# Moving the compressed-input, query and key projections between the quarters of a state space stage, with weight tiles of their own for the compression

## The chip, the cores and the metric

The kernel runs on one core of a Trainium2 chip. The metric is the device time of one execution in microseconds (us). The five instruction streams in the text are PE (TensorE, matrix products), ACT (ScalarE), DVE (VectorE), POOL (GpSimd) and SP (SyncE, which here only issues transfers).

## What is computed

One block of a hybrid model over 512 tokens of width 1024. A state space mixer and an attention mixer read the same normalized input, their outputs are gated and merged, then a convolutional feed-forward network, a gated extra input and a last norm follow. The part that the change touches is this, cut from the reference:

```python
n1 = rmsnorm(h, g_mix[i])
z = n1 @ w_in[i]
y_ssm = s5_mixer(z[..., OFF_SSM:OFF_Q], ...)
y_nsa = nsa_mixer(z[..., OFF_Q:OFF_KV], z[..., OFF_KV:OFF_NSA_GATE], ...)

def compress_blocks(k, pe, w1, w2):
    ch = k.reshape(bsz, g, t // CMP_STRIDE, CMP_STRIDE, dh)
    blocks = jnp.concatenate([ch[:, :, :-1], ch[:, :, 1:]], axis=3) + pe
    flat = blocks.reshape(bsz, g, blocks.shape[2], CMP_BLOCK * dh)
    return jax.nn.gelu(flat @ w1) @ w2

kc = compress_blocks(k_cmp, pe_k, wk1, wk2)
vc = compress_blocks(v_cmp, pe_v, wv1, wv2)
```

The projection z of the attention side has 128-column pieces for compressed keys and values, four for queries and two for the keys of the two other branches.

## The kernel before, in words

**Projections.** `proj` (its matmuls are lines 83 to 85) takes a 128-column piece of `w_in`, 512 KB in float32, loaded by `wraw` (L183) into a raw tile `wr`. ACT rounds it into a high part `wh` (L76) and DVE or POOL writes the rest into a low part `wl` (L55). PE then does 24 matmuls of 128x512: eight slices of the width, three products each. The result lies in a PSUM bank `pj` with the tag `acc`, which has two banks, until ACT has copied it on. The pool `weights` keeps three buffers of `wr` and two each of `wh` and `wl`. In the text the projections are numbered in the order in which PE does them: 0 to 3 are the inputs of the state space mixer, 4 and 5 the compressed keys and values, 6 to 9 the queries (`QT`), 10 and 11 the other keys (`KK`), 12 to 15 the first merge gates (`t1a`).

**The state space stage** is four calls of `ssm_quarter`. Each builds block matrices `Z` (DVE, copied by ACT) and `CX` (POOL, copied by ACT), transposes `Z` on PE (`wbps`, L641), copies the two results to `WB` (ACT), multiplies them with the inputs (`wps`, L649), multiplies `CX` and `Z` (`tps`, L669, into a bank that ACT first fills with zeros, L665), runs scans on DVE, and ends in the outputs `yps` (L703, L706). The matmuls of this stage are small: 32 to 128 columns.

**The compression** copies projections 4 and 5 from PSUM into `FL` (four ACT copies each), multiplies them with the weights `cmp_wk1` and `cmp_wv1` (`hps`, L748, 16 blocks each, 64 columns, plain float32), and applies a gelu and a second small product (`kps`, L756 and L767). Its four weight pieces of 512 KB take buffers of the same tag `wr` (L745, L746).

**What sets the order.** The Tile framework schedules: it takes the program order as priority, simulates the engines with its own durations, and writes one fixed order per engine. Each engine runs its own order one instruction after another and waits where a semaphore asks for it. So the program order is not the order on the engines: in the schedule of before, projections 4 to 15 already lie between the pieces of the quarters, although the text of the program has them behind `ssm_quarter(3)`.

Of the kernel before, what the change touches and what calls it, by code (L numbers as in the profile page):

```python
# [9 lines left out]
F32 = mybir.dt.float32  # L10
F32R = mybir.dt.float32r
# [5 lines left out]
MUL, ADD, SUB = ALU.mult, ALU.add, ALU.subtract  # L17

P = 128
T = 512  # L20
# [4 lines left out]
HD = 64  # L25
NCMP = 32
# [10 lines left out]
OFF_KV = 1024  # L37
# [8 lines left out]
def hybrid_kernel(ctx: ExitStack, tc: tile.TileContext, A, out):  # L46
    nc = tc.nc
    V, G, S, PE = nc.vector, nc.gpsimd, nc.scalar, nc.tensor

    def dr(name, off, ap):  # L50
        t = A[name]
        return bass.AP(tensor=t.tensor, offset=t.offset + off, ap=ap)

    def tt(o, a, b, op, e=V):
        e.tensor_tensor(o, a, b, op=op)  # L55
# [19 lines left out]
    def copy(o, a):  # L75
        S.activation(o, a, AF.Copy)  # L76

    def split(hi, lo, src, e=V):
        copy(hi, src)
        tt(lo, src, hi, SUB, e)  # L80

    def mm3(ps, lh, ll, rh, rl, start, stop):
        PE.matmul(ps, lh, rh, start=start, stop=False)  # L83
        PE.matmul(ps, lh, rl, start=False, stop=False)  # L84
        PE.matmul(ps, ll, rh, start=False, stop=stop)  # L85

    def pool(name, bufs=1, side=None, space=None):
        kw = {"name": name, "bufs": bufs, "reuse_waits": "tile"}
        if side:
            kw["side"] = side  # L90
        if space is not None:
            kw["space"] = space
        return tc.tile_pool(**kw)

    cp = ctx.enter_context(pool("const"))
    pn = ctx.enter_context(pool("norm"))
    pw = ctx.enter_context(pool("weights", 2))
# [3 lines left out]
    def bank(tag, name):  # L101
        return psp.tile([P, 512], F32, tag=tag, name=name, bufs=BANKS[tag])

    def slot(p, tag, shape, dt, name):
        return p.tile(shape, dt, tag=tag, name=name, bufs=1)
# [5 lines left out]
    def small(tag, n=1, bufs=4):  # L111
        return cp.tile([P, n], F32, name=tag, tag=tag, bufs=bufs)
# [58 lines left out]
    def last(engine):  # L171
        return next(i for i in reversed(nc.cur_bb.bb.instructions) if i.engine == engine)
# [3 lines left out]
    def either():  # L176
        turn[0] ^= 1
        return ("acc", "o")[turn[0]]
# [7 lines left out]
    def wload(name, ld, row0, c0, kt, c, e=V, keep=None, raw=None):  # L186
        if raw is None:
            raw = wraw(name, ld, row0, c0, kt, c)
        if keep is None:
            hi = pw.tile([P, kt * c], F32R, name="wh", tag="wh").rearrange("p (k c) -> p k c", k=kt)  # L190
            lo = pw.tile([P, kt * c], F32R, name="wl", tag="wl").rearrange("p (k c) -> p k c", k=kt)
        else:
            hi, lo = keep
        split(hi, lo, raw, e)
        return hi, lo

    def proj(c0, e=V, w=None):
        hi, lo = w or wload("w_in", INW, 0, c0, KD, P, e)
        ps = bank("acc", "pj")
        for k in range(KD):  # L200
            mm3(ps, hi[:, k], lo[:, k], n1h[:, k], n1l[:, k], k == 0, k == KD - 1)
        return ps
# [6 lines left out]
    pa = sA.enter_context(pool("attn_in"))  # L209
    sY = ExitStack()  # L210
    py = sY.enter_context(pool("ssm_out", 1, "right"))
    t1a = slot(py, "t8", [P, 4, T], F32, "t1a")
    sS = ExitStack()
    pS = sS.enter_context(pool("ssm", 1, "right"))
    Uc = pS.tile([P, NPAIR, NCH], F32, name="Uc")
# [113 lines left out]
    with tc.manual_schedule(engines={mybir.EngineType.PE, mybir.EngineType.Activation, mybir.EngineType.DVE}):  # L329
# [26 lines left out]
        r = rstd_of(ss4[:, 2:4], n=2)  # L356
# [163 lines left out]
    FL = slot(pa, "ptc", [P, 2, 16, 2, NCMP], F32, "FL")  # L520
# [33 lines left out]
    for lv in range(5):  # L554
        n = 1 << lv
# [8 lines left out]
    tab_at = last(mybir.EngineType.Pool)  # L564
# [3 lines left out]
    with tc.issue_after(tab_at):  # L568
# [12 lines left out]
        blk = pa.tile([P, 4], F32, name="blk")  # L581
# [6 lines left out]
    for ct in range(4):  # L588
# [3 lines left out]
        for j in range(L):  # L592
            n = L - 1 - j
# [8 lines left out]
    sM = ExitStack()  # L602
# [104 lines left out]
        stt(un, un, dcol[:, q:q + 1], yps, MUL, ADD)  # L707
        S.activation(yT[:, q].rearrange(flat), un, AF.Gelu_apprx_tanh)

    for q in range(4):  # L710
        ssm_quarter(q)
    sM.close()
    sS.close()


    KK = slot(pa, "kv", [P, 2, 2, T], F32R, "KK")
    KC = pa.tile([P, 2, 2, 64], F32R, name="KC")
    VC = slot(pa, "v4", [P, 2, 4, 2, HD], F32R, "VC")
    W2 = pa.tile([P, 2, HD], F32, name="W2")
    nc.sync.dma_start(W2[:, 0], dr("cmp_wk2", 0, [[HD, P], [1, HD]]))  # L720
    nc.sync.dma_start(W2[:, 1], dr("cmp_wv2", 0, [[HD, P], [1, HD]]))
    W2d = pa.tile([P, 2, HD], F32, name="W2d")
    G.tensor_copy(W2d, W2[:, 0:1].to_broadcast([P, 2, HD]))
    for i in range(2):
        ps = proj(OFF_KV + i * P)
        f = FL[:, i]
        for g in range(2):
            for j in range(2):
                x = ps[64 * g:64 * g + 64, j:j + 1]
                copy(f[64 * j:64 * j + 64, :, g, 0:NCMP - 1],  # L730
                     bass.AP(tensor=x.tensor, offset=x.offset, ap=[x.ap[0], [2, 16], [16, NCMP - 1]]))
    QT = slot(cp, "h16", [P, 4, 2, T], F32R, "QT")
    for i in range(4):
        ps = proj(OFF_Q + i * P)
        split(QT[:, i, 0], QT[:, i, 1], ps)
    for br, c0 in ((0, OFF_KV + 256), (1, OFF_KV + 512)):
        ps = proj(c0)
        for g in range(2):
            s0, o0 = 64 * g, 64 * (1 - g)
            copy(KK[s0:s0 + 64, br, g], ps[s0:s0 + 64])  # L740
            tt(KK[o0:o0 + 64, br, g], ps[s0:s0 + 64], KK[s0:s0 + 64, br, g], SUB)
    for i, nm in enumerate(("cmp_wk1", "cmp_wv1")):
        hps = bank("acc", "hps")
        for c in range(2):
            w1 = pw.tile([P, 8, P], F32, name="w1", tag="wr", bufs=3)  # L745
            nc.sync.dma_start(w1, dr(nm, c * 1024 * P, [[P, P], [P * P, 8], [1, P]]))  # L746
            for k in range(8):
                PE.matmul(hps[:, 0:64], w1[:, k], FL[:, i, 8 * c + k].rearrange("p g n -> p (g n)"),  # L748
                          start=(c == 0 and k == 0), stop=(c == 1 and k == 7))
        kps = bank("s", "kps")  # L750
        h1 = pa.tile([P, 64], F32, name=f"hid{i}")
        pe = small("pe")
        copy(pe, hps[:, NCMP - 1:NCMP])
        S.activation(h1, hps[:, 0:64], AF.Gelu_apprx_tanh, bias=pe)
        if i == 0:
            PE.matmul(kps[:, 0:64], W2d.rearrange("p a d -> p (a d)"), h1, start=True, stop=True)  # L756
            with tc.issue_after(tab_at):
                G.memset(KC.bitcast(F32), 0.0)
            kv = kps[:, 0:64].rearrange("p (g n) -> p g n", g=2)
            for s in range(2):  # L760
                r = slice(64 * s, 64 * s + 64)
                split(KC[r, 0, :, 32 * s:32 * s + 32], KC[r, 1, :, 32 * s:32 * s + 32], kv[r])
        else:
            hid = pw.tile([P, 2, 4, NCMP], F32, name="hidv", tag="mg")
            V.tensor_copy(hid, h1.rearrange("p (g n) -> p g n", g=2)[:, :, None].to_broadcast([P, 2, 4, NCMP]))
            for g in range(2):
                PE.matmul(kps[:, 64 * g:64 * g + 64], hid[:, g].rearrange("p r n -> p (r n)"), W2[:, 1],  # L767
                          start=True, stop=True)
                vc = pw.tile([P, 4, HD], F32, name="vc", tag="mg")
                tt(vc, kps[:, None, 64 * g:64 * g + 64].to_broadcast([P, 4, HD]),  # L770
                   blk[:, :, None].to_broadcast([P, 4, HD]), MUL)
                split(VC[:, g, :, 0], VC[:, g, :, 1], vc)


    t1s = [t1a]
# [25 lines left out]
    for hc in range(2):  # L801
        hi, lo = wload("ssm_w_glu", SSMW, 0, hc * 256, 4, 256, V)
        for cc in range(2):
            c = 2 * hc + cc
            ps = bank(either(), "glu")
# [15 lines left out]
    class Unit:  # L821
# [7 lines left out]
        def queries(self, prev):  # L829
            if self.br:  # L830
                self.QQ = prev.QQ
            else:
                self.QQ = pt.tile([P, 2, T], F32R, name="QQ", tag="QQ")
                for half in range(2):
                    nc.sync.dma_start(self.QQ[64 * half:64 * half + 64].bitcast(F32),
                                      QT[self.r0:self.r0 + 64, self.i].bitcast(F32))

        def scores(self, qt):
            w = P * (qt + 1)
            ps = bank("s", "sps")  # L840
            for x in range(2):
                PE.matmul(ps[:, :w], self.QQ[:, x, qt * P:(qt + 1) * P], KK[:, self.br, self.g, :w],
                          start=x == 0, stop=x == 1)
# [18 lines left out]
        def values(self, kt, prev):  # L862
            g = self.g
            if kt == NQ - 1:
                self.ops = prev.ops if self.br else bank("o", "ops")
                if not self.br:
                    vc = VC[:, g, self.h % 4].rearrange("p x d -> p (x d)")
                    PE.matmul(self.ops, vc, PTC[:, 0, g], start=True, stop=False)
# [9 lines left out]
    def compressed(qt):  # L878
        qs_ = slice(qt * P, (qt + 1) * P)
        ps = bank("s", "cs")  # L880
        for i in range(4):
            mm3(ps[:, 64 * i:64 * i + 64], QT[:, i, 0, qs_], QT[:, i, 1, qs_], KC[:, 0, i // 2], KC[:, 1, i // 2],
                True, True)
# [114 lines left out]
    for d2 in range(4):  # L998
        hi, lo = wload("w_br_nsa", D, 0, d2 * 256, 4, 256, V)
        for dd in range(2):  # L1000
            dt_ = 2 * d2 + dd
            ps = bank(either(), "br")
            for k in range(4):
                c = dd * P
                mm3(ps, hi[:, k, c:c + P], lo[:, k, c:c + P], oS[:, 0, k], oS[:, 1, k], k == 0, k == 3)
            mg = t2()[:, dt_]
# [20 lines left out]
    ps = bank("s", "cvps")  # L1027
# [8 lines left out]
    for qp in range(2):  # L1036
        for hf, qt in ((0, 0), (0, 1), (1, 0), (1, 1)) if qp == 0 else ((0, 2), (1, 2), (0, 3), (1, 3)):
            cs = slice(hf * 512, hf * 512 + 512)
            qs_ = slice(qt * P, (qt + 1) * P)
            ps = bank(either(), "wo")  # L1040
# [117 lines left out]
    with pool("fin", 1, "right") as pz:  # L1158
# [20 lines left out]
        for hf in range(2):  # L1179
            for qt in range(NQ):  # L1180
# [6 lines left out]
                for i, (c0, w) in enumerate(pieces):  # L1187
                    pg = bank(either(), "pg")
                    c = slice(c0, c0 + w)
# [14 lines left out]
                if hf == 1:  # L1204
                    xn = pw.tile([P, D], F32, name="xf", tag="wr", bufs=3)
                    r = rstd_of(ss[qt][:, 0:1], ss[qt][:, x:x + 1])
# [39 lines left out]
```

## Time and profile before

| | us |
|---|---|
| median of 3 runs | 847.91 |
| lowest, highest | 847.84, 849.98 |
| the profiled execution | 850.72 |
| its span, first to last instruction | 849.0 |
| PE busy in it | 825.2 |
| DVE, ACT, POOL busy | 454.2, 377.7, 278.8 |

The profile is one execution, 2.81 us above the median of the runs. Its page says of each engine how long it was busy. [...]

### The profile page before, as it was taken

How to read it: one execution, taken by the hardware profiler on the slowest of the kernel's cores; microseconds unless marked ns; L12 is line 12 of the kernel's file. 1: busy time of each engine (PE TensorE's matmuls, PEld its weight loads, DVE VectorE, ACT ScalarE, POOL GpSimd, SP SyncE). 2: the span in 40 equal slices, each digit the busy share in tenths (PEclk: the TensorE clock that was granted, in tenths of full speed). 3: DMA queues.
4: the chain of work that ended last, by engine and by line, in shares of the span. 5: the costliest groups of instructions: out<-in, count | busy, mean ns of one | idle time of the engine just before them, and what ended most of it. 6: DMA issues, size and time to landing. Idle time of an engine off the chain costs nothing. (4 is left out here: it accounts for less than half of the span.)

```text
span 849.0 us, 12151 instructions
## 1 busy us (share of the span) xinstructions
PE 825.2 (97%) x4565; PEld 688.9 (81%) x4565; DVE 454.2 (53%) x968; ACT 377.7 (44%) x688; POOL 278.8 (33%) x314
## 2 busy tenths in 40 slices
PE   7998999999999999999999999999999999999996
PEld 5876888888888888878898888888888888888885
DVE  6898877348676750595454444444444212324535
ACT  4447533344776663344354444444444212333522
POOL 7485200214555444141033333333333221221341
PEclk9998998899999999999999999999999999999998
DMA  9363223531332522344032333333332223541202
GB/s 243 85 167 88 63 64 90 151 97 51 100 91 63 170 54 76 104 133 135 1 100 75 100 99 100 100 99 100 99 93 92 90 99 100 183 164 50 73 22 80
DMA packets 112000, 83.66 MB, mean 99 GB/s; under 512 B 9665, under 2 KB 97477, under 8 KB 111942
## 3 DMA queue, kind: packets, MB, share of 16 engines
q1 hardware_dynamic: 111262, 81.82, 33.3%
q10 hardware_dynamic: 680, 1.07, 0.3%
q8 instruction: 36, 0.59, 0.3%
q14 instruction: 22, 0.18, 0.1%
HBM read 75.54 MB, written 3.15 MB: 93 GB/s over the span
## 5 line engine op out<-in xcount | busy, mean ns | idle before, releaser
L55 POOL TENSOR_TENSOR wl<-wr,wh 128x1024 fp32r<-128x1024 f32 x49 | 118.2, 2413 | 346.2 <-ACT wh L76 320.5
L76 ACT ACTIVATE wh<-wr 128x1024 fp32r<-128x1024 f32 x101 | 106.8, 1058 | 124.8 <-PE dn L85 47.0
L55 DVE TENSOR_TENSOR wl<-wr,wh 128x1024 fp32r<-128x1024 f32 x52 | 66.8, 1284 | 87.7 <-ACT wh L76 87.7
L83 PE MATMUL pj<-n1h,wh 128*128 128x512 f32 x224 | 93.1, 416 | 0.8 <-ACT wh L76 0.8
L85 PE MATMUL pj<-n1h,wl 128*128 128x512 f32 x224 | 89.4, 401 | 0.2 <-DVE wl L55 0.2
L84 PE MATMUL pj<-n1l,wh 128*128 128x512 f32 x224 | 89.3, 399 | 0.0
L64 DVE SCALAR_TENSOR_TENSOR cv<-ub,cvp,cv 128x511 f32<-128x511 f32 (+1 forms) x44 | 32.9, 748 | 70.6 <-ACT cv L1075 69.8
L84 PE MATMUL ua<-n2l,wh 128*128 128x512 f32 (+1 forms) x176 | 67.0, 381 | 0.4 <-DVE n2l L64 0.4
L83 PE MATMUL ua<-n2h,wh 128*128 128x512 f32 (+1 forms) x176 | 67.0, 380 | 0.2 <-ACT n2h L167 0.2
L83 PE MATMUL ub<-n2h,wh 128*128 128x512 f32 (+1 forms) x176 | 66.8, 379 | 0.0
L84 PE MATMUL ub<-n2l,wh 128*128 128x512 f32 (+1 forms) x176 | 66.8, 379 | 0.0
L85 PE MATMUL ub<-n2h,wl 128*128 128x512 f32 (+1 forms) x176 | 66.8, 379 | 0.0
L85 PE MATMUL ua<-n2h,wl 128*128 128x512 f32 (+1 forms) x176 | 66.8, 379 | 0.0
L84 PE MATMUL dn<-wl,ffh 128*128 128x512 f32 x168 | 66.0, 393 | 0.0
L85 PE MATMUL dn<-wh,ffl 128*128 128x512 f32 x168 | 65.6, 391 | 0.0
L83 PE MATMUL dn<-wh,ffh 128*128 128x512 f32 x168 | 57.4, 391 | 0.0
L85 PEld LDWEIGHTS pj<-n1h,wl 128*128 128x128 f32 x224 | 42.9, 192 | 10.1 <-DVE wl L55 0.6
L83 PEld LDWEIGHTS pj<-n1h,wh 128*128 128x128 f32 x224 | 43.1, 193 | 9.5 <-ACT wh L76 1.6
L61 POOL TENSOR_SCALAR pr<-pr,su,gates 128x512 f32<-128x512 f32 (+1 forms) x64 | 38.7, 615 | 36.7 <-DVE su L849 35.6
L84 PEld LDWEIGHTS pj<-n1l,wh 128*128 128x128 f32 x224 | 43.3, 193 | 7.4
L76 ACT ACTIVATE ffh<-cv 128x512 fp32r<-128x512 f32 x22 | 13.9, 632 | 68.0 <-POOL cv L55 68.0
L55 DVE TENSOR_TENSOR ffl<-cv,ffh 128x512 fp32r<-128x512 f32 x22 | 15.2, 693 | 51.1 <-ACT ffh L76 51.1
(407 smaller groups left out, 1899.6 us busy)
## 6 DMA issues: line engine op xcount, KB each, us to landing
wr<-in_w_up_dram SPq DMA_DIRECT2D x44, 512.0 KB, 4.3
wr<-in_w_in_dram SPq DMA_DIRECT2D x28, 512.0 KB, 3.9
wr<-in_w_down_dram SPq DMA_DIRECT2D x22, 512.0 KB, 3.5
QQ<-QT SPq DMA_DIRECT2D x16, 256.0 KB, 3.6
wr<-in_w_out_dram SPq DMA_DIRECT2D x8, 512.0 KB, 4.4
wr<-in_w_ple_gate_dram SPq DMA_DIRECT2D x8, 512.0 KB, 4.2
xall<-in_x_dram SPq DMA_DIRECT2D x4, 512.0 KB
wr<-in_w_br_ssm_dram SPq DMA_DIRECT2D x4, 512.0 KB
```

Source lines behind the costliest of these rows:

```text
L55: e.tensor_tensor(o, a, b, op=op)
L61: e.tensor_scalar(o, a, s1, s2, op0=op0, op1=op1)
L64: e.scalar_tensor_tensor(o, a, s, b, op0=op0, op1=op1)
L76: S.activation(o, a, AF.Copy)
L83: PE.matmul(ps, lh, rh, start=start, stop=False)
L84: PE.matmul(ps, lh, rl, start=False, stop=False)
L85: PE.matmul(ps, ll, rh, start=False, stop=stop)
```

## The change

The projections are written in another place of the program: 4 and 5 ahead of the four quarters, the queries 6 and 7 behind quarter 0, 8 and 9 behind quarter 1, the keys 10 and 11 behind quarter 2. The compression stands behind quarter 3, as before. Three of its four weight pieces get tiles of their own: both pieces of `cmp_wk1` in `wk1`, which lies in the slot `t8` (before it, the raw tile `wv1` of the value columns lies there, after it `t1a`), and the first piece of `cmp_wv1` in the slot `v4` (later `VC`). They are loaded at the head of the program part. The fourth stays in a `wr` buffer. The amount of work is the same on every engine.

```diff
-    t1a = slot(py, "t8", [P, 4, T], F32, "t1a")
...
-    for q in range(4):
-        ssm_quarter(q)
-    sM.close()
-    sS.close()
...
+    def w1load(nm, c, t):
+        nc.sync.dma_start(t, dr(nm, c * 1024 * P, [[P, P], [P * P, 8], [1, P]]))
+        return t
+
+    wk1 = slot(py, "t8", [P, 2, 8, P], F32, "wk1")
+    wv1 = slot(pa, "v4", [P, 8, P], F32, "wv1c")
+    w1s = [[w1load("cmp_wk1", c, wk1[:, c]) for c in range(2)], [w1load("cmp_wv1", 0, wv1)]]
...
+    def compress(i):
         hps = bank("acc", "hps")
         for c in range(2):
-            w1 = pw.tile([P, 8, P], F32, name="w1", tag="wr", bufs=3)
-            nc.sync.dma_start(w1, dr(nm, c * 1024 * P, [[P, P], [P * P, 8], [1, P]]))
+            if c == len(w1s[i]):
+                w1s[i].append(w1load("cmp_wv1", 1, pw.tile([P, 8, P], F32, name="w1", tag="wr", bufs=3)))
             for k in range(8):
-                PE.matmul(hps[:, 0:64], w1[:, k], FL[:, i, 8 * c + k].rearrange("p g n -> p (g n)"),
+                PE.matmul(hps[:, 0:64], w1s[i][c][:, k], FL[:, i, 8 * c + k].rearrange("p g n -> p (g n)"),
...
+    for i in range(2):
+        compress_in(i)
+    for q in range(4):
+        ssm_quarter(q)
+        if q < 2:
+            queries(2 * q)
+            queries(2 * q + 1)
+        elif q == 2:
+            keys(0)
+            keys(1)
+    compress(0)
+    VC = compress(1)
+    sM.close()
+    sS.close()
+    t1a = slot(py, "t8", [P, 4, T], F32, "t1a")
```

`compress_in`, `queries` and `keys` hold the loops that stood behind the quarters, unchanged. How the schedule moved is shown at three places.

**ACT in quarter 0.** Before, from the copies of the second `Z` to the second `WB` (`WB_857` and `WB_864` are the two of quarter 0):

```order
L76 ACTIVATE Z_800<-z_1000 64x16x16 x2
L76 ACTIVATE WB_857<-wbps 128x512
L76 ACTIVATE CX_803<-x_845 64x20x16 x2
L76 ACTIVATE Z_801<-z_1007 64x16x16 x2
L665 ACTIVATE tps<-ident 128x512
L76 ACTIVATE wh<-wr 128x1024
L76 ACTIVATE FL<-pj 64x16x31 x4
L76 ACTIVATE WB_864<-wbps 128x512
```

Now, over the same work (`WB_940` and `WB_947` are the two):

```order
L76 ACTIVATE Z_799<-z_1149 64x16x16 x2
L76 ACTIVATE CX_802<-x_928 64x20x16 x2
L76 ACTIVATE wh<-wr 128x1024
L76 ACTIVATE FL<-pj 64x16x31 x4
L76 ACTIVATE Z_800<-z_1156 64x16x16 x2
L76 ACTIVATE WB_940<-wbps 128x512
L76 ACTIVATE CX_803<-x_1163 64x20x16 x2
L664 ACTIVATE tps<-ident 128x512
L76 ACTIVATE wh<-wr 128x1024
L76 ACTIVATE FL<-pj 64x16x31 x4
L76 ACTIVATE WB_947<-wbps 128x512
```

The first `WB` stood ahead of the next `wh` and of the `FL` copies; now a `wh` and the `FL` copies of projection 4 stand ahead of the first `WB`, and a `wh` and those of projection 5 ahead of the second.

**SP, the loads from the second half of the quarters on.** Before (`w_1810` to `w_1852` are the compression weights, the last `wr` are projections 12 to 15):

```order
L183 DMA wr<-in_w_in_dram 128x8x128 x3
L746 DMA w_1810<-in_cmp_wk_dram 128x8x128
L615 DMA un<-ud 128x512
L746 DMA w_1820<-in_cmp_wk_dram 128x8x128
L746 DMA w_1842<-in_cmp_wv_dram 128x8x128
L615 DMA un<-ud 128x512 x2
L746 DMA w_1852<-in_cmp_wv_dram 128x8x128
L183 DMA wr<-in_w_in_dram 128x8x128 x4
```

Now (`w_1847` is the one piece of compression weights left here):

```order
L183 DMA wr<-in_w_in_dram 128x8x128 x3
L722 DMA w_1847<-in_cmp_wv_dram 128x8x128
L183 DMA wr<-in_w_in_dram 128x8x128
L614 DMA un<-ud 128x512
L183 DMA wr<-in_w_in_dram 128x8x128 x2
L614 DMA un<-ud 128x512
L183 DMA wr<-in_w_in_dram 128x8x128
L614 DMA un<-ud 128x512
L183 DMA wr<-in_ssm_w_glu_dram 128x4x256 x2
```

Before, the four gate loads stood behind the last compression weight; now they stand in the middle of the quarters, and the one piece left stands ahead of them.

**SP, the loads ahead of the quarters.** Before:

```order
L183 DMA wr<-in_w_in_dram 128x8x128
L720 DMA W_1531<-in_cmp_wk_dram 128x64
L721 DMA W_1531<-in_cmp_wv_dram 128x64
L183 DMA wr<-in_w_in_dram 128x8x128 x2
L591 DMA ud<-un 128x512
```

Now:

```order
L183 DMA wr<-in_w_in_dram 128x8x128
L711 DMA W_821<-in_cmp_wk_dram 128x64
L712 DMA W_821<-in_cmp_wv_dram 128x64
L722 DMA wv1c<-in_cmp_wv_dram 128x8x128
L722 DMA wk_830<-in_cmp_wk_dram 128x8x128 x2
L183 DMA wr<-in_w_in_dram 128x8x128 x2
L590 DMA ud<-un 128x512
```

Three pieces of 512 KB came in ahead of the loads of projections 3 and 4.

## Rows read from the trace of the kernel before

**Rows 1.** The page: busy us, share of the span, instructions of each engine.

```profile
PE 825.2 (97%) x4565; PEld 688.9 (81%) x4565; DVE 454.2 (53%) x968; ACT 377.7 (44%) x688; POOL 278.8 (33%) x314
```

**Rows 2.** Waits of PE, whole run: us in total, times, longest.

```profile
PE wps L649 <- ACT WB L76: 2.9, 1, 2.9
PE hps L748 <- DMA w<-in_cmp_wv_dram: 1.3, 1, 1.3
```

**Rows 3.** Windows: length, busy (count) PE, PEld, DVE, ACT, POOL, PEclk, DMA share, GB/s.

```profile
68.10:72.50 4.40, 1.13 (x35) 0.81 (x34) 4.33 (x6) 4.32 (x8) 1.34 (x2) 0.91 0.00 1
72.50:78.60 6.10, 6.08 (x43) 5.06 (x44) 3.65 (x8) 3.15 (x7) 2.34 (x4) 0.50 0.34 88
128.90:142.00 13.10, 13.10 (x231) 12.15 (x230) 10.93 (x25) 4.10 (x8) 0.00 (x0) 1.00 0.25 70
143.30:153.60 10.30, 9.44 (x29) 7.73 (x30) 3.13 (x7) 2.71 (x5) 2.37 (x1) 0.51 0.72 185
```

**Rows 4.** Timeline of PE, 49 to 79 us: start, length, instruction, [idle before].

```profile
49.63 0.39 PE L85 MATMUL pj<-n1h,wl 128*128 128x512 f32 x1
...
55.52 0.39 PE L84 MATMUL pj<-n1l,wh 128*128 128x512 f32 x1
...
72.52 2.08 PE L649 MATMUL wps<-Uc,WB 128*128 128x128 f32 x8 [2.86 <-ACT WB L76]
```

**Rows 5.** Timeline of ACT, 65 to 72 us, same columns.

```profile
65.89 0.95 ACT L76 ACTIVATE CX<-x 64x320 f32<-64x320 f32 x2
67.05 0.85 ACT L76 ACTIVATE Z<-z 64x256 f32<-64x256 f32 x2 [0.21 <-DVE z L55]
67.92 0.60 ACT L665 ACTIVATE tps<-ident 128x512 f32<-128x512 f32 x1
68.55 1.06 ACT L76 ACTIVATE wh<-wr 128x1024 fp32r<-128x1024 f32 x1
69.51 2.33 ACT L76 ACTIVATE FL<-pj 64x496 f32<-64x496 f32 x4
71.87 0.60 ACT L76 ACTIVATE WB<-wbps 128x512 f32<-128x512 f32 x1
```

**Rows 6.** Timeline of PE, 143 to 149 us.

```profile
143.33 3.65 PE L748 MATMUL hps<-FL,w 128*128 128x64 f32 x16 [1.26 <-DMA w<-in_cmp_wv_dram]
...
148.77 0.80 PE L83 MATMUL pj<-n1h,wh 128*128 128x512 f32 x1 [0.83 <-ACT wh L76]
```

**Rows 7.** Timeline of the SP queue, 137 to 148 us.

```profile
137.81 0.38 SPq L746 DMA_DIRECT2D w<-in_cmp_wv_dram  x1
139.60 8.41 SPq L183 DMA_DIRECT2D wr<-in_w_in_dram  x4
```

**Rows 8.** Timeline of ACT, 141 to 149 us.

```profile
145.06 1.06 ACT L76 ACTIVATE wh<-wr 128x1024 fp32r<-128x1024 f32 x1 [2.73 <-DMA wr<-in_w_in_dram]
```

**Rows 9.** Timeline of DVE, 25 us.

```profile
25.23 2.63 DVE L55 TENSOR_TENSOR WV<-wv,WV 128x1024 fp32r<-128x1024 f32 x2
```

**Rows 10.** Timeline of the SP queue, 29 us.

```profile
29.02 4.16 SPq L183 DMA_DIRECT2D wr<-in_w_in_dram  x2
```

**Rows 11.** DMA issues, 20 to 150 us: count, size, median us to landing.

```profile
wr<-in_w_in_dram SPq DMA_DIRECT2D x13, 512.0 KB, 4.2
```

**Rows 12.** Windows, columns as in rows 3.

```profile
24.00:29.00 5.00, 4.07 (x32) 3.85 (x31) 4.97 (x5) 2.43 (x3) 4.58 (x8) 1.00 0.02 5
```

**Rows 13.** Timeline of ACT, 44 us.

```profile
44.44 1.06 ACT L76 ACTIVATE wh<-wr 128x1024 fp32r<-128x1024 f32 x1 [1.09 <-PE pj L84]
```

**Rows 14.** Timeline of PE, 114 to 118 us.

```profile
114.63 0.65 PE L706 MATMUL yps<-sr,CX 128*32 128x128 f32 x16
...
117.17 1.16 PE L649 MATMUL wps<-Uc,WB 128*128 128x128 f32 x8
```

**Rows 15.** Timeline of ACT, 109 to 111 us.

```profile
109.99 1.06 ACT L76 ACTIVATE wh<-wr 128x1024 fp32r<-128x1024 f32 x1 [2.64 <-PE pj L84]
110.95 0.58 ACT L76 ACTIVATE QT<-pj 128x512 fp32r<-128x512 f32 x1
```

More of the change, by code (lines that the diff above doesn't have):

```diff
@@ L708, in ssm_quarter @@
         S.activation(yT[:, q].rearrange(flat), un, AF.Gelu_apprx_tanh)
-    for q in range(4):
-        ssm_quarter(q)
-    sM.close()
-    sS.close()
-    KK = slot(pa, "kv", [P, 2, 2, T], F32R, "KK")
-    KC = pa.tile([P, 2, 2, 64], F32R, name="KC")
-    VC = slot(pa, "v4", [P, 2, 4, 2, HD], F32R, "VC")
     W2 = pa.tile([P, 2, HD], F32, name="W2")
@@ L723, in hybrid_kernel, with compress_in @@
     G.tensor_copy(W2d, W2[:, 0:1].to_broadcast([P, 2, HD]))
-    for i in range(2):
+    KK = slot(pa, "kv", [P, 2, 2, T], F32R, "KK")
+    KC = pa.tile([P, 2, 2, 64], F32R, name="KC")
+    QT = slot(cp, "h16", [P, 4, 2, T], F32R, "QT")
+    with tc.issue_after(tab_at):
+        G.memset(KC.bitcast(F32), 0.0)
+    def w1load(nm, c, t):
[4 more added lines that the diff above has]
+    w1s = [[w1load("cmp_wk1", c, wk1[:, c]) for c in range(2)], [w1load("cmp_wv1", 0, wv1)]]
+    def compress_in(i):
         ps = proj(OFF_KV + i * P)
-        f = FL[:, i]
         for g in range(2):
@@ L729, in hybrid_kernel, with queries, keys @@
                 x = ps[64 * g:64 * g + 64, j:j + 1]
-                copy(f[64 * j:64 * j + 64, :, g, 0:NCMP - 1],
+                copy(FL[64 * j:64 * j + 64, i, :, g, 0:NCMP - 1],
                      bass.AP(tensor=x.tensor, offset=x.offset, ap=[x.ap[0], [2, 16], [16, NCMP - 1]]))
-    QT = slot(cp, "h16", [P, 4, 2, T], F32R, "QT")
-    for i in range(4):
+    def queries(i):
         ps = proj(OFF_Q + i * P)
         split(QT[:, i, 0], QT[:, i, 1], ps)
-    for br, c0 in ((0, OFF_KV + 256), (1, OFF_KV + 512)):
-        ps = proj(c0)
+    def keys(br):
+        ps = proj(OFF_KV + 256 + 256 * br)
         for g in range(2):
@@ L741, in hybrid_kernel @@
             tt(KK[o0:o0 + 64, br, g], ps[s0:s0 + 64], KK[s0:s0 + 64, br, g], SUB)
-    for i, nm in enumerate(("cmp_wk1", "cmp_wv1")):
+    def compress(i):
         hps = bank("acc", "hps")
         for c in range(2):
-            w1 = pw.tile([P, 8, P], F32, name="w1", tag="wr", bufs=3)
-            nc.sync.dma_start(w1, dr(nm, c * 1024 * P, [[P, P], [P * P, 8], [1, P]]))
+            if c == len(w1s[i]):
+                w1s[i].append(w1load("cmp_wv1", 1, pw.tile([P, 8, P], F32, name="w1", tag="wr", bufs=3)))
             for k in range(8):
-                PE.matmul(hps[:, 0:64], w1[:, k], FL[:, i, 8 * c + k].rearrange("p g n -> p (g n)"),
+                PE.matmul(hps[:, 0:64], w1s[i][c][:, k], FL[:, i, 8 * c + k].rearrange("p g n -> p (g n)"),
                           start=(c == 0 and k == 0), stop=(c == 1 and k == 7))
@@ L756, in hybrid_kernel @@
             PE.matmul(kps[:, 0:64], W2d.rearrange("p a d -> p (a d)"), h1, start=True, stop=True)
-            with tc.issue_after(tab_at):
-                G.memset(KC.bitcast(F32), 0.0)
             kv = kps[:, 0:64].rearrange("p (g n) -> p g n", g=2)
@@ L762, in hybrid_kernel @@
                 split(KC[r, 0, :, 32 * s:32 * s + 32], KC[r, 1, :, 32 * s:32 * s + 32], kv[r])
[L763 to L772, printed above, removed]
+            return None
+        VC = slot(pa, "v4", [P, 2, 4, 2, HD], F32R, "VC")
+        hid = pw.tile([P, 2, 4, NCMP], F32, name="hidv", tag="mg")
+        V.tensor_copy(hid, h1.rearrange("p (g n) -> p g n", g=2)[:, :, None].to_broadcast([P, 2, 4, NCMP]))
+        for g in range(2):
+            PE.matmul(kps[:, 64 * g:64 * g + 64], hid[:, g].rearrange("p r n -> p (r n)"), W2[:, 1],
+                      start=True, stop=True)
+            vc = pw.tile([P, 4, HD], F32, name="vc", tag="mg")
+            tt(vc, kps[:, None, 64 * g:64 * g + 64].to_broadcast([P, 4, HD]),
+               blk[:, :, None].to_broadcast([P, 4, HD]), MUL)
+            split(VC[:, g, :, 0], VC[:, g, :, 1], vc)
+        return VC
+    for i in range(2):
[13 more added lines that the diff above has]
+    t1a = slot(py, "t8", [P, 4, T], F32, "t1a")
     t1s = [t1a]
```

## The prediction

> **What bounds the kernel now.** I read the page first, then the waits of PE, then windows around the places that they name, then the timelines. The page says that PE is busy in 97% of the span [rows 1]: 849.0 - 825.2 leaves 23.8 us idle, and only a part of that lies in the stage that the change touches. So the change cannot win by taking work off another engine; it can only shorten waits of PE, or the time that PE works at its lower clock. The waits show two of size in this stage: `wps` for a `WB` copy of ACT, 2.9 us, and `hps` for compression weights, 1.3 us [rows 2]. [...]
>
> Call the first place A, in quarter 0, and the second B, the compression.
>
> **A before.** ACT copied the last `FL` piece of projection 4 until 71.8 and only then the second `WB` (71.87 to 72.47); PE stood 2.86 us for it and began `wps` at 72.52 [rows 4, 5]. Then 6.08 us of busy time ran at 0.50 [rows 3], which at full clock are 3.0 us: a loss of 3.0.
>
> **B before.** The second half of the value weights was issued at 137.81, once a raw buffer had come free, and the four gate loads stood behind it in the queue from 139.60 on [rows 7]. PE waited 1.26 us for those weights and 0.83 us for the high part of a gate projection [rows 6]; that high part began at 145.06, after ACT had waited 2.73 us for its transfer [rows 8]. With the 9.44 us of busy time at 0.51 [rows 3], worth 4.6 us, B costs 1.26 + 0.83 + 4.6 = 6.7 us.
>
> **The change, part by part.**
>
> *B, the weights and the gate loads.* Three of four weight pieces are now loaded ahead of the quarters, the fourth in the middle of them, and the gate loads right behind it. In the new order ACT rounds projections 12 and 13 before the compression's gelu, 12 even before the copies of `KK` of projection 10. Both waits of B lose their cause, and with no gap the clock has no reason in these rows to fall: -6.7 us. What is late next there is the low part of projection 13 on POOL, which has all of the `hps` time ahead of it. The fourth piece holds one of three raw buffers until the `hps` end, so projections 12 to 15 rotate through two; each then waits for the low part two projections back, which is done in time, and if that cover were gone it would cost one landing, 4.2 us [rows 11].
>
> *A, the order of ACT.* This part loses. Before, the first `WB` stood ahead of the `FL` copies. Now, from the end of the second `CX` pair (65.89 + 0.95 = 66.84), ACT does a `wh` 1.06, `FL` 2.33, `Z` 0.85, the first `WB` 0.60, `CX` 0.95, the zero fill 0.60, `wh` 1.06, `FL` 2.33 and the second `WB` 0.60, all from [rows 5]: 10.4 us, so the second `WB` is ready at 77.2 in place of 72.5, 4.7 us later. PE has more to put in front of it: 34 projection matmuls (24 of projection 5 and 10 of projection 6) where it had 17. The 17 more take 0.227 us each (27 rows from 49.63 to 55.52 [rows 4], 5.89 over 26 steps), 3.9 us in all. Projection 6 has to wait for the bank of projection 4, which the first `FL` copies free at about 70.2, but that only moves idle time within A. Net: 4.7 - 3.9 = +0.8 us of waiting. The gap is again close to 3 us (the last `tps` piece can end at about 74.3), so I take the clock price of before, 3.0, again. It is not known; its bounds are 0, if the several gaps keep it up (-3.0), and twice, if it falls a second time (+3.0). I take one fall, because the gap just ahead of the `wps` is the row that it is nearest to, 2.86 us.
>
> [...]
>
> *The loads ahead of the quarters.* The buffer of `wk1` is free once DVE has read the value columns, 25.23 + 2.63 = 27.9 [rows 9]. SP's next issue before was at 29.02 [rows 10], so it is hardly held up. The transfer engines were 0.02 busy from 24 to 29 us [rows 12]. Projection 3's load now has two pieces ahead of it: at worst 29.02 + 3 x 4.2 = 41.6 [rows 10, 11], and ACT takes it at 44.44 [rows 13]. Projections 4 and later have more room. Cost 0; without this cover, up to 4.2.
>
> *Projections in quarters 1 to 3.* PE already had projections between the pieces of the quarters; the number on each engine is the same, and a few moved by a place or two. PE shows no larger wait there [rows 2], so 0. The slot of `t1a`, freed later, is written first by projection 12, behind the `hps`: 0.
>
> **Sum.** -6.7 + 0.8 = -5.9 us. Against the profiled execution that is 850.72 - 5.9 = 844.8 (span 843.1). The median lies 2.81 us below that execution; carried over it gives 847.91 - 5.9 = 842.0 us.
>
> **The rivals.** A difference below 0.3%, 2.5 us, cannot be told from no change here.
>
> 1. *A keeps its clock* (its gaps lie apart): -8.9, 839.0 us. Against it: 2.86 us idle was enough before [rows 3, 4]. 12%.
> [...]
> 3. *B's clock falls without a gap*: the stretch of small matmuls now takes in the last 16 `hps` matmuls too, so it is longer than 13.10 us. The slow time then costs its 4.6 again: -1.3, 846.6 us. Against it: 13.10 us at 1.00 [rows 3]. 8%.
> 4. *The change does not do what it says*: the schedule had the projections in the quarters already, and if B's slow time has another cause than the two waits, nothing moves: 847.9 us. 6%.
> 5. *Slower: ACT's line repeats in quarters 1 to 3.* There PE now goes from a whole projection straight to `wbps`, `wps` and `yps`, and ACT has the next `wh` (1.06) and the projection's copy (0.58) [rows 15] ahead of the second `WB` (0.60): 2.2 us, which PE covers with 2.54 us of `yps` (114.63 to 117.17) and 1.16 of the first `wps` [rows 14], 3.7 in all. If ACT is later than that by over 1.5 us, each quarter pays what A paid, 2.86 + 3.0 = 5.9. From two quarters on it outweighs the gain: -5.9 + 11.8, 853.8 us. 5%.
>
> **How the numbers follow.** My forecast has the remaining 60%. Faster by over 0.3%: the forecast, 1 and 2, 0.60 + 0.12 + 0.09 = 0.81. Within: 3 and 4, 0.14. Slower: 5, 0.05. The range goes from rival 1 with half a microsecond to spare, 838.5, to rival 3, 846.7; it leaves out 4 and 5, 11%, and what strays beyond its ends.
>
> **What would show it.** B right: no wait of PE for compression weights or for a gate's high part, and a clock of 1.00 over the whole compression and projection 12. A right: a wait of `wps` for `WB` of about 3 us that ends near 77 us, a shorter wait of projection 6 that ends near 70 us, and one window at about 0.50 for some 6 us of busy time. Quarters 1 to 3 right: no wait of PE above 0.5 us there. I would be wrong if the clock falls in the compression without a gap, if A shows two low windows or none, or if any wait of `wps` for `WB` appears after quarter 0.

## The result, and the profile after

| | before | after |
|---|---|---|
| median, us | 848.89 (4 runs) | 842.84 (4 runs) |
| lowest, highest | 847.84, 849.98 | 842.56, 843.92 |
| span of the profiled execution | 849.0 | 840.9 |
| PE busy in it | 825.2 | 818.3 |

The ratio is 0.9931, with a 95% interval of 0.9912 to 0.995: faster by 0.7%, some 6 us. The page of the changed kernel (busy us, and the granted clock in 40 slices, in tenths of full speed) answers to [rows 1]:

```profile
span 840.9 us, 12149 instructions
PE 818.3 (97%) x4565; PEld 684.1 (81%) x4565; DVE 453.0 (54%) x968; ACT 377.0 (45%) x688; POOL 279.2 (33%) x314
...
PEclk9999999999999999999999999999999999999999
```

Of the 8.1 us between the two spans, 6.9 are PE busy time and only 1.2 are idle time (23.8 before, 840.9 - 818.3 = 22.6 now). PE issues the same 4565 matmuls; it was busy for less time because it worked less of it at its lower clock (the mean granted clock is 0.987 before and 0.998 now, as a share of full speed). The waits of PE (us in total, times, longest) answer to [rows 2]:

```profile
PE gb L331 <- DMA wv<-in_g_mix_dram: 4.7, 1, 4.7
PE wps L648 <- ACT WB L76: 2.6, 1, 2.6
PE pj L83 <- ACT FL L76: 1.3, 1, 1.3
...
PE pj L83 <- ACT un L76: 0.4, 1, 0.4
```

The waits for compression weights and for a gate's `wh` are gone, and the one wait of A has become two. Windows of the changed kernel, with the columns of [rows 3] (PEclk is the granted clock as a share of full speed, the DMA share that in which the transfer engines were busy): the work between the two gaps of A, the second gap, the time behind it, the compression, and the window that stood at 0.51 in [rows 3].

```profile
70.00:74.50 4.50, 4.44 (x50) 3.66 (x50) 1.54 (x4) 4.35 (x9) 1.96 (x4) 1.00 0.44 120
74.50:77.10 2.60, 0.04 (x1) 0.00 (x0) 2.16 (x3) 2.54 (x6) 1.54 (x1) 1.00 0.14 25
77.10:80.80 3.70, 3.69 (x47) 3.12 (x48) 2.50 (x5) 2.21 (x5) 2.32 (x3) 1.00 0.43 124
126.90:142.00 15.10, 15.10 (x249) 14.17 (x248) 11.57 (x27) 4.70 (x12) 2.36 (x1) 1.00 0.21 54
143.30:153.60 10.30, 10.30 (x125) 8.58 (x124) 5.22 (x10) 2.01 (x4) 0.00 (x0) 1.00 0.30 101
```

In this execution the clock is 1.00 in all of them, at A too. The two gaps on the timeline of PE (compare [rows 4]; in brackets how long PE had been idle, and what released it):

```profile
70.06 0.50 PE L83 MATMUL pj<-n1h,wh 128*128 128x512 f32 x1 [1.32 <-ACT FL L76]
...
77.11 1.16 PE L648 MATMUL wps<-Uc,WB 128*128 128x128 f32 x8 [2.56 <-ACT WB L76]
```

The timeline of ACT over the same time (compare [rows 5]) shows who held PE up: the second `WB` comes behind a `wh` and the `FL` copies of projection 5.

```profile
67.68 2.33 ACT L76 ACTIVATE FL<-pj 64x496 f32<-64x496 f32 x4
70.04 0.84 ACT L76 ACTIVATE Z<-z 64x256 f32<-64x256 f32 x2
70.91 0.60 ACT L76 ACTIVATE WB<-wbps 128x512 f32<-128x512 f32 x1
...
73.14 1.06 ACT L76 ACTIVATE wh<-wr 128x1024 fp32r<-128x1024 f32 x1
74.10 2.33 ACT L76 ACTIVATE FL<-pj 64x496 f32<-64x496 f32 x4
76.46 0.60 ACT L76 ACTIVATE WB<-wbps 128x512 f32<-128x512 f32 x1
```

The SP queue (compare [rows 7, 10]): two pieces of `wk1` go out right ahead of the pair of loads that began at 29.02 before and begins at 28.95 now, and the last gate load is out at 129.42, where all four gate loads began at 139.60 before.

```profile
27.80 1.00 SPq L722 DMA_DIRECT2D wk<-in_cmp_wk_dram  x2
28.95 4.06 SPq L183 DMA_DIRECT2D wr<-in_w_in_dram  x2
...
92.22 0.37 SPq L722 DMA_DIRECT2D w<-in_cmp_wv_dram  x1
...
109.64 6.44 SPq L183 DMA_DIRECT2D wr<-in_w_in_dram  x2
...
129.42 0.37 SPq L183 DMA_DIRECT2D wr<-in_w_in_dram  x1
```

### The profile page after: what moved, and what is told of

Read it like the earlier page. It is cut to its first block, busy times and chain, and to the rows that moved or that the text cites. A ratio compares the mean times of both kernels' runs of the same rounds, so it can differ in the third digit from the quotient of the medians.

```text
span 840.9 us, 12149 instructions
## 1 busy us (share of the span) xinstructions
PE 818.3 (97%) x4565; PEld 684.1 (81%) x4565; DVE 453.0 (54%) x968; ACT 377.0 (45%) x688; POOL 279.2 (33%) x314
```

## The experiments

The theory: the gain is B, the weights in tiles of their own; the move of the projections costs a little at A; the clock is what makes the sums uncertain. The rivals: the place of the projections makes the gain, or the clock does. In what follows, a fall is a stretch in which the granted clock is 0.5 in place of 1.00; its price is an estimate, half of PE's busy time in it. Before, the 128x512 matmuls in the fall of A began 0.43 us apart (76.97, 77.40 and 77.83 on the timeline of PE), 1.9 times the 0.227 us at 1.00 (from [rows 4]). Each kernel was timed against the kernel before on the same chip.

**The kernel before once more** (no edit).

> The kernel before, unchanged, to see whether its two slow stretches (A in quarter 0, B in the compression) come in every execution. The times of before so far lie in two groups, 847.9 and 849.9. Theory: both falls of the clock come every time, since the gaps ahead of them are fixed by the schedule; then every execution shows the same mean clock, 0.987, and the times within 0.3%. Rival: a fall is decided anew in each execution; then an execution without the fall at A is about 3.0 us shorter with a mean clock higher by 3.0/849 = 0.0036, and the two groups of times differ by that much in clock too.

Measured: 848.42 us median of 12 executions, from 847.64 to 850.67, ratio 0.9997 (0.9986 to 1.0007). 23 executions of the kernel before, timed beside it, lie between 846.38 and 850.91, with mean clocks from 0.986 to 0.994. Neither side is right as put: the mean clocks differ, but neither profile is without a fall at A and B. Both places fell in the new profile too, but for another length:

```profile
72.60:76.20 3.60, 3.60 (x38) 3.10 (x38) 1.68 (x4) 0.93 (x3) 2.33 (x3) 0.53 0.56 149
144.40:151.40 7.00, 5.80 (x13) 4.12 (x14) 2.29 (x4) 1.59 (x3) 2.37 (x1) 0.51 0.69 188
```

Added up over windows of 0.2 us, the clock was low at A for 3.4 us, where it was low for 6.8 in the first profile (0.8 of them in the gap, where nothing ran), and at B for 6.8 in place of 10.2. The price of a fall thus differs between executions of one and the same program: 1.7 or 3.0 us at A. The first profiled execution, 850.72, was one of the dearest.

The waits at B are not the same either. In this profile `hps` does not wait for compression weights at all; PE waits twice for a gate projection, 2.6 us in all, where it waited 1.26 + 0.83 = 2.1 us in the first:

```profile
144.36 0.79 PE L83 MATMUL pj<-n1h,wh 128*128 128x512 f32 x1 [1.38 <-ACT pe L76]
...
146.78 0.79 PE L83 MATMUL pj<-n1h,wh 128*128 128x512 f32 x1 [1.20 <-ACT wh L76]
```

The view puts the first of these down to a small copy of ACT (0.15 us from 144.22); that copy stood right behind the high part of projection 12 (143.26 to 144.32), for whose transfer ACT had waited 2.05 us. So the late gate loads behind the last compression weight are in both profiles, the late compression weight only in one.

**Only the weights.** The change, with the projections written behind the quarters:

```diff
-    for i in range(2):
-        compress_in(i)
     for q in range(4):
         ssm_quarter(q)
-        if q < 2:
-            queries(2 * q)
-            queries(2 * q + 1)
-        elif q == 2:
-            keys(0)
-            keys(1)
+    for i in range(2):
+        compress_in(i)
+    for i in range(4):
+        queries(i)
+    for i in range(2):
+        keys(i)
     compress(0)
```

> Only the weights: three of the four compression pieces in tiles of their own and loaded early, the projections written behind the four quarters as before. Theory (the gain is B's two waits and its slow clock, 6.7 us, and the move of the projections gains nothing by itself): 848.9 - 6.7 = 842.2 us, with no wait for compression weights or for a gate's high part and a clock of 1.00 over the compression, and A as before (a wait for the second WB of about 2.9 us). Rival (the gain of the change comes from the place of the projections): 847 us or more, with a slow stretch left in the compression.

Measured: 842.42 us median (842.14 to 842.68), ratio 0.9925 (0.9911 to 0.994), 5.9 us below the 848.32 of before. Its waits show none for compression weights or for `wh`, and A's is as before; its windows show a low clock at A and 1.00 over the compression:

```profile
PE wps L648 <- ACT WB L76: 2.9, 1, 2.9
```

```profile
72.40:76.00 3.60, 3.43 (x38) 3.16 (x38) 1.58 (x4) 0.94 (x3) 2.33 (x3) 0.53 0.55 150
128.90:152.00 23.10, 23.10 (x356) 20.82 (x355) 15.50 (x34) 6.85 (x15) 2.28 (x1) 1.00 0.22 61
```

In this profile B is gone and A is left, and the weights alone give the whole gain.

**Only the place.** The change, with all four pieces in raw buffers:

```diff
-    wk1 = slot(py, "t8", [P, 2, 8, P], F32, "wk1")
-    wv1 = slot(pa, "v4", [P, 8, P], F32, "wv1c")
-    w1s = [[w1load("cmp_wk1", c, wk1[:, c]) for c in range(2)], [w1load("cmp_wv1", 0, wv1)]]
+    w1s = [[], []]
...
-                w1s[i].append(w1load("cmp_wv1", 1, pw.tile([P, 8, P], F32, name="w1", tag="wr", bufs=3)))
+                w1s[i].append(w1load(("cmp_wk1", "cmp_wv1")[i], c, pw.tile([P, 8, P], F32, name="w1", tag="wr", bufs=3)))
```

> Only the place: the projections between the quarters as in the change, all four weight pieces in raw buffers and loaded at the compression as before. Theory: B stays (a wait for weights or for a gate's high part, a clock near 0.5 behind it, 6.7 us in all); A costs 1.0 us more of waiting (3.9 in place of 2.9) and, if its clock holds as in the profile of the change, 3.0 less: 848.9 + 1.0 - 3.0 = 846.9, and 849.9 if the clock of A falls. Rival (the place alone removes B, because the projections are done earlier): 843 us or less.

Measured: 847.08 us median of 12, ratio 0.9982 (0.9968 to 0.9995), from 845.5 (mean clock 0.996) to 849.52 (0.988). Its timeline of PE has the two gaps of A of the change, and at B two waits for the high part of a gate:

```profile
69.87 0.50 PE L83 MATMUL pj<-n1h,wh 128*128 128x512 f32 x1 [1.29 <-ACT FL L76]
...
76.92 2.07 PE L648 MATMUL wps<-Uc,WB 128*128 128x128 f32 x8 [2.57 <-ACT WB L76]
...
145.09 0.50 PE L83 MATMUL pj<-n1h,wh 128*128 128x512 f32 x1 [0.60 <-ACT wh L76]
...
147.14 0.50 PE L83 MATMUL pj<-n1h,wh 128*128 128x512 f32 x1 [1.32 <-ACT wh L76]
```

The place does not remove B: 0.60 + 1.32 us of waits, and a low clock behind them. And here, behind the same gaps at A behind which the first profile of the change kept its clock, it fell:

```profile
76.20:83.20 7.00, 6.28 (x46) 5.18 (x47) 4.02 (x8) 2.88 (x7) 2.32 (x3) 0.51 0.28 75
...
147.80:151.40 3.60, 3.60 (x11) 2.79 (x10) 0.85 (x3) 0.00 (x0) 1.75 (x1) 0.53 0.74 174
```

The median is still 1.2 us below that of before, though the waits are not shorter: 1.29 + 2.57 + 0.60 + 1.32 = 5.8 us here, 2.86 + 2.1 = 5.0 and 2.86 + 2.6 = 5.5 in the two profiles of before. The times go with the mean clock: five executions at 845.5 to 845.85 have 0.996, three at 847.07 to 847.28 have 0.993 or 0.994, two near 848.3 have 0.990 and two near 849.4 have 0.988. So what the place gains by itself is most likely clock; where it gains it is not shown, since only one of the twelve was profiled.

**The change, three times more** (no edit).

> The changed kernel, unchanged, for a second profile and more executions. Its waits at A are fixed by the order (1.3 and 2.6 us). Theory: whether the clock falls behind them is decided anew in each execution, since the place-only kernel had the same two gaps (1.29 and 2.57 us) and a low stretch of 6.9 us behind them, while the first profile of the change had none; then most executions lie at 842.5 to 843.0 and some 1.3 to 3 us above. Rival: in this kernel the clock never falls at A; then all executions lie within 0.5 us of 842.7.

> The changed kernel again, for one more profile. Of ten executions so far some three lie 1.3 to 1.7 us above the others. Theory: those are executions in which the clock fell at A for 3.4 us (1.7 us of work lost) with the same two gaps of 1.3 and 2.6 us; a profile that shows the low stretch has a time near 844.4, one that does not lies near 842.8. Rival: the slower executions are late for another cause (the first loads of the kernel); then a profile near 844.4 shows no low stretch, or one near 842.8 does.

> As the run before it: one more profile of the changed kernel, near 844.4 with a low stretch at A or near 842.8 without.

Measured: 843.04 us median of six (842.46 to 844.57; ratio 0.9931, 0.9915 to 0.9948), profile without a fall at A; then, on another chip, 844.41 and 844.46 (two executions each; ratios 0.9948 and 0.9949, intervals from 0.9928 to 0.9969) with a fall at A in both profiles. The time behind the second gap in the first of these runs, without a fall:

```profile
77.20:80.60 3.40, 3.32 (x45) 2.83 (x46) 2.13 (x4) 2.14 (x6) 2.31 (x3) 1.00 0.46 134
```

The first of the two with a fall:

```profile
77.11 1.95 PE L648 MATMUL wps<-Uc,WB 128*128 128x128 f32 x8 [2.54 <-ACT WB L76]
```

```profile
77.20:80.60 3.40, 3.40 (x40) 3.01 (x40) 1.50 (x3) 0.74 (x3) 2.32 (x3) 0.51 0.39 116
```

The first profile of the change began this `wps` at the same 77.11, after 2.56 us of idle time, and kept its clock. Of 14 executions seven lie between 842.46 and 843.07, with mean clocks of 0.997 or 0.998, one at 843.92 with 0.996, and six between 844.26 and 844.66 with 0.994 to 0.996. The six lie 1.6 us above the 842.8 of the first seven; half of 3.4 us is 1.7. The theory holds where profiles reach: the two near 844.3 (844.34 and 844.26) have the fall, the two near 842.7 (842.56 and 842.84) have not.

**The weights alone, once more** (no edit).

> The weights-only kernel once more, for a second profile of an undivided gap of 2.86 us at A. Theory: behind the undivided gap the clock falls every time (three profiles out of three so far), so all executions lie at 842.1 to 842.9 or above and the profile shows a low stretch of 3 us or more at A. Rival: it is decided anew here too; then some executions lie near 840.8, the 1.7 us of a 3.4 us stretch at half clock below 842.4.

Measured: 842.42 us median (842.18 to 842.61), ratio 0.9918 (0.9904 to 0.9933), 6.9 us below before, and again a low clock of 3.4 us at A:

```profile
72.40:76.00 3.60, 3.60 (x39) 2.95 (x39) 1.89 (x3) 1.05 (x4) 2.32 (x3) 0.53 0.49 141
```

All ten executions of this kernel lie between 842.14 and 842.68, none near the 840.8 of the rival. Behind the undivided gap of 2.86 us the clock fell in all five profiles that have this gap (the two of before, these two, and the kernel with both inputs behind quarter 0, below).

**Tiles of their own for the key weights only.**

```diff
-    wv1 = slot(pa, "v4", [P, 8, P], F32, "wv1c")
-    w1s = [[w1load("cmp_wk1", c, wk1[:, c]) for c in range(2)], [w1load("cmp_wv1", 0, wv1)]]
+    w1s = [[w1load("cmp_wk1", c, wk1[:, c]) for c in range(2)], []]
...
-                w1s[i].append(w1load("cmp_wv1", 1, pw.tile([P, 8, P], F32, name="w1", tag="wr", bufs=3)))
+                w1s[i].append(w1load("cmp_wv1", c, pw.tile([P, 8, P], F32, name="w1", tag="wr", bufs=3)))
```

> The change with tiles of their own for the two key pieces alone; both value pieces in raw buffers again. They then hold two of the three raw buffers until the compression's matmuls are done, and the gate projections rotate through one. Theory (B's gain needs the raw buffers free for the gate loads): a wait of PE for a gate's high part of about 1 us comes back, often with a low clock behind it, 843.8 to 845.5 us. Rival (it was the loads of the weights that were late, and one queue place ahead of the gates is enough): no such wait, 842.8 us as the change.

Measured: 844.61 us median (844.47 to 844.66), ratio 0.9944 (0.9929 to 0.9959). The time is where the theory put it, for a reason that it did not give. There is no wait at B: the value weights are out at 93.34 and the last gate load at 140.90, and the windows show 1.00 over the compression.

```profile
93.34 5.36 SPq L722 DMA_DIRECT2D w<-in_cmp_wv_dram  x2
...
140.90 0.37 SPq L183 DMA_DIRECT2D wr<-in_w_in_dram  x1
```

```profile
77.20:80.60 3.40, 3.40 (x40) 2.85 (x40) 1.67 (x3) 0.84 (x3) 2.32 (x3) 0.52 0.39 118
128.90:152.00 23.10, 23.10 (x296) 20.49 (x299) 16.57 (x36) 6.78 (x16) 1.98 (x1) 1.00 0.29 81
```

What it shows is a fall at A for 3.4 us, behind gaps of 1.28 and 2.57 us: it has the time of the change's executions with that fall. In this profile two pieces taken out of the raw buffers are enough to cure B, with both value pieces ahead of the gate loads; so the rival is right on the wait, and wrong on the time. The third tile removes no wait that these profiles show.

**Both compressed inputs behind quarter 0.**

```diff
-    for i in range(2):
-        compress_in(i)
     for q in range(4):
         ssm_quarter(q)
+        if q == 0:
+            for i in range(2):
+                compress_in(i)
```

> The change, but with both compressed inputs behind quarter 0. On ACT the first WB stands ahead of both FL groups again, the second behind the first group, as in the kernel before. Theory (the place of queries and keys is worth nothing, that of the inputs sets A): A as before, one wait of about 2.9 us and a low stretch, B as in the change: 842.4 us like the weights-only kernel. Rival (queries and keys between the quarters are worth something by themselves): over 1 us below or above that with A unchanged.

Measured: 842.82 us median (841.93 to 844.14), ratio 0.9925 (0.991 to 0.994). A is as before, a wait of 2.86 us and a low clock behind it, here for 6.8 us, and the clock is 1.00 over the compression:

```profile
70.80:77.80 7.00, 5.73 (x43) 4.73 (x44) 4.57 (x9) 4.11 (x10) 2.32 (x3) 0.51 0.28 77
128.90:152.00 23.10, 23.10 (x348) 20.57 (x352) 19.04 (x40) 7.13 (x17) 2.04 (x2) 1.00 0.22 60
```

Where queries and keys stand makes no difference that these runs can tell.

**The second compressed input alone behind quarter 0**, run twice.

```diff
-    for i in range(2):
-        compress_in(i)
+    compress_in(0)
     for q in range(4):
         ssm_quarter(q)
+        if q == 0:
+            compress_in(1)
```

> The change, but with the second compressed input (projection 5) written behind quarter 0, so that on ACT both WB copies of quarter 0 stand ahead of its FL copies. PE then has one gap at A, from the end of projection 5 near 68.7 to the first WB near 71.5, about 2.8 us, in place of two of 1.3 and 2.6. Theory 1 (one gap of that length with little work ahead of it drops the clock, as before, and two shorter ones do not): 842.8 - 1.1 + 3.0 = 844.7 with a window near 0.50 behind the gap. Theory 2 (the length of the gap does not decide): 842.8 - 1.1 = 841.7, with 1.00 throughout. Rival for the waits: the gap only moves to tps or projection 6, and the idle time stays 3.9 us.

> The kernel with the second compressed input behind quarter 0 once more, for its distance from the change. Theory (its gain is the 2.5 us of waiting at A that it does not have, 1.4 in place of 3.9): 840.0 us, no low stretch at A, 2.5 to 3 us below the change. Rival (its first four executions were lucky in the clock): a median near 841.7, some executions higher by 1.7 us.

Measured: 840.01 (839.44 to 840.44) and 839.95 us (839.84 to 840.04), ratios to before 0.9897 (0.988 to 0.9913) and 0.9896 (0.988 to 0.9913). This is the fastest version, 2.8 us below the 842.84 of the change, and 4.5 us below the four executions of the change that were timed beside its second run (844.26 to 844.66), which lie where those with a fall at A lie. On ACT, both `WB` copies stand ahead of the second `FL` group:

```profile
67.78 2.33 ACT L76 ACTIVATE FL<-pj 64x496 f32<-64x496 f32 x4
70.14 0.84 ACT L76 ACTIVATE Z<-z 64x256 f32<-64x256 f32 x2
71.00 1.09 ACT L76 ACTIVATE WB<-wbps 128x512 f32<-128x512 f32 x2
...
74.69 2.33 ACT L76 ACTIVATE FL<-pj 64x496 f32<-64x496 f32 x4
```

On PE one gap is left, and `wps` and `tps` run through behind it:

```profile
70.17 0.50 PE L83 MATMUL pj<-n1h,wh 128*128 128x512 f32 x1 [1.42 <-ACT FL L76]
...
73.03 1.95 PE L648 MATMUL wps<-Uc,WB 128*128 128x128 f32 x16
74.91 1.96 PE L668 MATMUL tps<-CX,Z 128*32 128x32 f32 x64
```

The expectation was too dear by 1.4 us of waiting: it had PE idle until the first `WB`, but 12 matmuls of projection 6 begin at 70.17 and last beyond the end of both copies, 71.00 + 1.09 = 72.1. Idle time at A is 1.4 in place of 3.9 us, which is 2.5 of the 2.8 us gained; with the 1.7 us of a fall it makes 4.2 of the 4.5. With one gap of this length the clock stayed up in both profiles:

```profile
72.50:78.60 6.10, 6.10 (x92) 5.35 (x91) 3.79 (x6) 5.93 (x12) 3.85 (x4) 1.00 0.28 76
```

All eight executions lie between 839.44 and 840.44, none near the 841.7 of the rival.

## Why the prediction was right, and which step was not

842.0 was forecast, within 838.5 to 846.7, and 842.84 measured; "faster" was right. The forecast stood on a median of 847.91 for before; with a fourth run that median is 848.89. As a difference 5.9 us was forecast and 6.05 measured.

- **B: right.** "Both waits of B lose their cause", -6.7: the weights alone gave -5.9 and -6.9 us in two comparisons. The cause is shown from both sides: in the three profiles with waits at B (two of before, one of the place alone) the clock fell behind them, and in the ten profiles without these waits it was 1.00 through the compression. Of the two waits that the text names, the one for the compression weights is there in one profile of three, the one for a gate's high part in all. Rival 3, a fall without a gap, did not come: 15.10 us of the compression at 1.00 in the profile after, 23.10 in that of the weights alone.
- **A, the waits: right.** 0.8 us more was forecast, with the second `WB` ready at 77.2 and projection 6 held up until about 70.2. They came at 77.06 (76.46 + 0.60) and 70.06, and the idle time went from 2.86 to 1.32 + 2.56 = 3.88, 1.0 more.
- **A, the clock: wrong as a step.** "I take one fall", 3.0 us, was taken because the gap ahead of the `wps` is near 2.86 us. The text named "two low windows or none" as what would refute it, and the first profile shows none, which is rival 1. Four profiles of the change show none, none, 3.4 us and 3.4 us; the price is 0 or 1.7 us, not 3.0. The 0.09 in the sum of the chances stands for a second fall at A, which no run shows: of the six profiles with two gaps at A, four show one fall and two show none.
- **Why the sum still came out.** The clock prices were read from one execution, and a dear one: 3.0 at A and 4.6 at B, where the second profile of before has half of 3.4, 1.7, at A and 5.80 x 0.49 = 2.8 at B (with its waits of 2.6, B costs 5.4 there in place of 6.7). So the two first profiles differ by more (8.1 us in span, near rival 1's 8.9) than the medians (6.05 us, near the forecast's 5.9): the first execution of before paid more for its clock than the second, and that of the change paid nothing at A. Two errors of size, a price too high for B and one too high for A's fall in the change, work against each other in the sum: the first makes the gain too large, the second too small. That the median comes within 0.2 us of the forecast difference is in part luck.
- **The move as a whole:** the change against the weights alone is 843.04 - 842.42 = +0.6 us in runs timed side by side, where +0.8 was forecast. Two things lie behind it: 1.0 us more of waiting, and a fall of the clock that is paid for in fewer executions. The medians are too near each other for a finer account.
- **Loads ahead of the quarters, quarters 1 to 3: right.** The pair of loads behind the weights went out at 28.95 (29.02 before), and the wait of `wps` for `WB` is there once, in quarter 0, so rival 5 is out. Rival 4 falls with the measured gain.

## What to carry over

When a profile shows a wait for a buffer's turn, look at what stands behind that load in its queue: taking three pieces out of the rotating buffers removed waits of 2.1 to 2.6 us and the low clock that followed, together 5.9 and 6.9 us in two comparisons; two pieces were enough to remove the waits. On an engine that serves two chains, as ACT does here, look at the order of its copies: moving one group of `FL` copies behind the `WB` copies that PE waits for is worth another 2.8 us, and 4.5 us against executions in which the clock fell. And read the price of a clock fall from more than one execution, with the times of all runs beside it.

## What was not expected of the hardware

The schedule alone does not fix whether the clock falls. The change had gaps of 1.28 to 1.32 and 2.54 to 2.56 us at A in all four profiles, and the clock fell to 0.5 behind them in two; the place-only and the key-weights kernel have these gaps within 0.03 us, and it fell in both. Nor is the length of the low stretch fixed: 3.4 and 6.8 us at A of the kernel before, 6.8 and 10.2 at B. Nor does the time from the first instruction fix it: two profiles of the change have the same `wps` at 77.11 us, and behind it the clock is 1.00 in one and 0.51 in the other. What decides it in a given execution stays open: no run here varied it by itself. One thing more stays open: the five executions of the key-weights kernel lie within 0.2 us of each other at 844.6, as if all of them had the fall. Their mean clocks, 0.994 to 0.996, are those of the change's slower executions, but a mean clock does not say where the clock was low (two executions of the fastest version have 0.996 at 839.44 and 840.17 us), and only one of the five was profiled.
